# Decay, rate and gate products and head sums of an RWKV-7 block: full-precision products exchanged for products of split parts

## The chip, the cores and the metric

The program runs on one core of a Trainium2 chip. The metric is the time of one execution on the device, in microseconds. The engines are TensorE (PE, with its weight loads listed apart as PEld), VectorE (DVE), ScalarE (ACT), GpSimd (POOL) and SyncE (SP), which issues most transfers. Each engine takes its instructions strictly in the order in which they stand in its queue.

## The reference

Two transformer blocks on 256 tokens of width 2048, in float32: the first with RWKV-7 time mixing, a causal multi-scale pooling path, a feed-forward part and a gated side input, the second with gated linear attention, sparse attention and a feed-forward part. The change touches only these lines of the first block:

```python
w = -jax.nn.softplus(-(w0 + jnp.tanh(zw) @ w_up)) - 0.5      # decay, rank 64
decay = jnp.exp(-jnp.exp(w))
a = jax.nn.sigmoid(a0 + za @ a_up)                           # rate, rank 64
g = jax.nn.sigmoid(zg) @ g_up                                # gate, rank 160
...
y = wkv7_scan(r_h, hs(decay), k_h, v_h, -kk, kk * a_h)       # state 64x64 a head, 16 heads
...
y = y + jnp.sum(r_h * k_h * r_k, axis=-1, keepdims=True) * v_h
return y.reshape(B, T, RWKV_WIDTH) * g, v_first
```

## The kernel before

**Main products in split parts.** Every large weight is read in pieces of 128x1024 f32 ("halves" here: eight 128x128 blocks). `stream` (L236 to L246) takes such a piece from one of five `raw` slots (tile r), into which SyncE loads it, casts it on ACT to the reduced type fp32r (L241, tile h, one of three `hi` slots) and subtracts on DVE what was lost (L245, tile l, one of three `lo` slots; in the time-mix stage every eighth subtraction goes to POOL). Activations are split likewise (xh, xl). `gemm_a` (L251 to L267) then makes three products for each block, at L263, L264 and L265: h with xh, h with xl, l with xh. A half is thus 24 products of 128x128 weights with 256 columns. A slot comes free when its last reader is done, and slots are given out in a fixed order that the scheduler sets when the program is built; so is the order of every engine's queue.

**The time-mix stage** (`block1_mix`) first makes the three tiles of low-rank activations (`rwkv_lora`: wa of 64 decay rows over 64 rate rows, and sg of 128 and 32 gate rows), then walks over eight tiles of 128 channels (two heads each). For a tile, `rwkv_front` makes the r, k and v products (six halves) and the head norm, multiplies the small decay and rate weights (`lora`, 64 rows each) with wa in full f32 at L361 by the helper `mm`, and sums r*k over each head by a product of the constant `same` with rkk, also f32. For every pair of tiles, `rwkv_inverse` makes 31 dependent pairs of DVE steps (L524 a product xt, L526 an addition to X) between transfers through device memory, and ends with a transpose (L539) and some small products; `rwkv_chain` walks over four chunks (small products at L361, L582 and L585, copies on ACT, the update of S on DVE at L588). `rwkv_post` normalises Y, multiplies the small gate weights (`lorag`, 128 rows and 32 rows) with sg in f32 into a bank of `acc` that stays reserved for it, and writes the split result. The order of these pieces is written in `block1_mix`: the inverse and chain of one pair stand beside the main products of the next tiles, and the last pair beside the pooling path (`pool_path`, L640 to L651), which has eight tiles of main products of its own.

**Small weights.** Before, `lora` and `lorag` have buffers of their own, two each, filled by transfers that ACT issues (L402 and L599).

Of the kernel before, what the change touches and what calls it, by code (L numbers as in the profile page):

```python
# [10 lines left out]
F32 = mybir.dt.float32  # L11
F32R = mybir.dt.float32r
# [8 lines left out]
T = 256  # L21
# [81 lines left out]
def arrays_of(inputs):  # L103
    f = np.float32
    g = {k: np.asarray(v) for k, v in inputs.items()}
# [13 lines left out]
    lora = np.zeros((8, 128, 384), f)  # L119
    lora[:, :64, :128] = g["w_up"][0].reshape(64, 8, 128).transpose(1, 0, 2)  # L120
    lora[:, 64:, :128] = g["a_up"][0].reshape(64, 8, 128).transpose(1, 0, 2)
    lora[:, :, 128:256] = g["g_up"][0][:128].reshape(128, 8, 128).transpose(1, 0, 2)
    lora[:, :32, 256:384] = g["g_up"][0][128:].reshape(32, 8, 128).transpose(1, 0, 2)
# [46 lines left out]
class Kern:  # L170
# [51 lines left out]
    def head_rsqrt_rows(self, psum, pool, r):  # L222
        nc = self.nc
        x = pool.tile([128, 2, 2, 64], F32, name="hx", tag="hx")
# [153 lines left out]
    def rwkv_lora(self, act):  # L378
# [4 lines left out]
        wa = self.shifted(L, first[0], self.p("mu_wa"), "wa", bufs=1)  # L383
        nc.scalar.activation(wa[:64], wa[:64], AF.Tanh)
        sg = []
        for q in range(2):
            z = self.shifted(L, first[1 + q], self.p("mu_g", q), f"g{q}", bufs=1)
            nc.scalar.activation(z, z, AF.Tanh, scale=0.5)
            nc.vector.tensor_scalar(z, z, 0.5, 0.5, ALU.mult, ALU.add)
            sg.append(z)  # L390
        self.wa, self.sg = wa, sg
# [6 lines left out]
    def rwkv_front(self, j, act):  # L398
        nc, w = self.nc, self.I["w_in"]
        F, S = self.fp, self.store  # L400
        lora = F.tile([128, 128], F32, name="lora", tag="lora", bufs=2)
        nc.scalar.dma_start(lora, self.I["lora"][j, :, :128])  # L402
# [58 lines left out]
        inv = self.head_rsqrt_rows(self.fr, F, hr)  # L461
# [18 lines left out]
        self.mm(ps[:, :T], self.c("same"), rkk)  # L480
# [111 lines left out]
    def rwkv_post(self, tiles, mix, bank=None):  # L592
# [4 lines left out]
        for i, d in enumerate(tiles):  # L597
            lora = C.tile([128, 256], F32, name="lorag", tag="lorag", bufs=2)
            nc.scalar.dma_start(lora, self.I["lora"][d["j"], :, 128:])  # L599
            loras.append(lora)  # L600
            Y8 = d["Y"][64:].rearrange("p c h i -> p (c h) i")
            sq = C.tile([128, 8, 64], F32, name="psq", tag="psq")
# [5 lines left out]
        for i, d in enumerate(tiles):  # L608
            j, Y, lora = d["j"], d["Y"], loras[i]
# [8 lines left out]
            y = C.tile([128, T], F32, name="y", tag="y")  # L618
# [829 lines left out]
```

## Time and profile before

| | us |
|---|---|
| median of 3 runs | 2444.03 |
| lowest and highest of them | 2443.96 and 2447.99 |
| the profiled execution, its own time | 2445.46 |
| the profiled execution, span of the trace | 2443.7 |

The span runs from the first to the last instruction that the trace holds, and the execution's own time has 1.8 us around it. In the trace a busy time is the sum of the instructions of an engine, overlaps counted once; a row of a group gives how many there were, their sum and the mean of one, and then how long the engine was idle ahead of them and what ended that. PE's products are pipelined, so the length of one in the trace (0.28 us for 128x256) is longer than the distance from one start to the next, and it is the distance that counts. A product in full f32 has two records (x2), one in the split type has one.

### The profile page before, as it was taken

Reading aid. Unit: us, or ns where it says so; the run is one execution under the profiler, and the core shown is the slowest. Engines: PE = TensorE matmul, PEld = TensorE weight load, DVE = VectorE, ACT = ScalarE, POOL = GpSimd, SP = SyncE. Lnnn points to the kernel's source line nnn. Section 1 sums busy time; section 2 is a strip of 40 time slices with the busy share of each in tenths; the row PEclk is TensorE's granted clock in tenths of the full one; section 3 lists DMA queues with packets and bytes.
Section 4 is the critical chain, followed back from the end, with each engine's and each line's share of the span. In section 5 each row is a group of like instructions: output and inputs, shape, how many; then the busy total and the mean of one; then the engine's idle time right before and its main releaser. Section 6 shows DMA issues by size and latency. Waiting matters only on the chain.

```text
span 2443.7 us, 33752 instructions
## 1 busy us (share of the span) xinstructions
PE 2419.5 (99%) x12882; PEld 2045.0 (84%) x12882; DVE 1515.5 (62%) x2313; ACT 1160.4 (47%) x1654; POOL 200.0 (8%) x323
## 2 busy tenths in 40 slices
PE   9999999999999999999999999999999999999999
PEld 8988878888888888888888798888888888888887
DVE  7788866555555555556676577865555455555555
ACT  5554445444444444444565466545443434444443
POOL 1543320000000000000000044200000000000000
PEclk9999999999999999999999999999999999999999
DMA  6443336555555555556556543255555555555554
GB/s 231 159 134 113 107 103 239 185 185 190 189 190 190 189 189 190 190 188 237 183 185 237 193 149 121 94 192 185 187 189 197 183 196 189 190 190 189 190 191 162
DMA packets 135378, 439.14 MB, mean 180 GB/s; under 512 B 26784, under 2 KB 29216, under 8 KB 134064
## 3 DMA queue, kind: packets, MB, share of 16 engines
q1 hardware_dynamic: 130032, 423.58, 51.8%
q10 hardware_dynamic: 5184, 13.41, 1.4%
q8 instruction: 101, 1.65, 0.3%
q14 instruction: 61, 0.50, 0.1%
HBM read 429.59 MB, written 7.34 MB: 179 GB/s over the span
## 4 chain that ended last, share of the span: by engine, by line
PE 95%; DVE 3%; ACT 1%; issue 1%; DMA 0%; POOL 0%; SPq 0%; ACTq 0%; DVEq 0%
PE acc L741 24%; PE acc L740 24%; PE acc L742 24%; PE acc L263 4%; PE acc L264 4%; PE acc L265 4%; PE ch L361 3%; PE fr L361 2%; PE fr L879 1%; DVE l L245 1%; PE fr L782 1%; PE acc L361 1%; PE ch L582 0%; PE ch L585 0%; DVE xt L524 0%
## 5 line engine op out<-in xcount | busy, mean ns | idle before, releaser
L245 DVE TENSOR_TENSOR l<-r,h 128x1024 fp32r<-128x1024 f32 x774 | 951.6, 1230 | 772.1 <-ACT h L241 768.7
L241 ACT CAST h<-r 128x1024 fp32r<-128x1024 f32 x780 | 820.1, 1052 | 977.6 <-PE acc L742 813.9
L741 PE MATMUL acc<-l,qh 128*128 128x512 f32 x1472 | 579.4, 394 | 0.0
L742 PE MATMUL acc<-h,ql 128*128 128x512 f32 x1472 | 574.7, 390 | 0.0
L740 PE MATMUL acc<-h,qh 128*128 128x512 f32 x1472 | 521.6, 392 | 0.0
L741 PE MATMUL acc<-l,xh 128*128 128x512 f32 x1120 | 438.9, 392 | 0.0
L742 PE MATMUL acc<-h,xl 128*128 128x512 f32 x1120 | 436.7, 390 | 0.0
L740 PE MATMUL acc<-h,xh 128*128 128x512 f32 x1120 | 396.3, 391 | 0.0
L742 PEld LDWEIGHTS acc<-h,ql 128*128 128x128 f32 x1472 | 277.2, 188 | 56.3
L741 PEld LDWEIGHTS acc<-l,qh 128*128 128x128 f32 x1472 | 277.0, 188 | 56.3
L740 PEld LDWEIGHTS acc<-h,qh 128*128 128x128 f32 x1472 | 275.3, 188 | 57.2 <-issue 0.2
L741 PEld LDWEIGHTS acc<-l,xh 128*128 128x128 f32 x1120 | 210.4, 188 | 43.6
L742 PEld LDWEIGHTS acc<-h,xl 128*128 128x128 f32 x1120 | 210.5, 188 | 42.7
L740 PEld LDWEIGHTS acc<-h,xh 128*128 128x128 f32 x1120 | 209.7, 188 | 42.9
L265 PE MATMUL acc<-xh,l 128*128 128x256 f32 x512 | 149.2, 291 | 0.8 <-DVE l L245 0.6
L264 PE MATMUL acc<-xl,h 128*128 128x256 f32 x512 | 149.2, 291 | 0.0
L263 PE MATMUL acc<-xh,h 128*128 128x256 f32 x512 | 148.4, 290 | 0.0
L265 PE MATMUL acc<-qh,l 128*128 128x256 f32 x416 | 120.9, 291 | 0.2 <-DVE l L245 0.2
L263 PE MATMUL acc<-qh,h 128*128 128x256 f32 x416 | 121.2, 291 | 0.0
L264 PE MATMUL acc<-ql,h 128*128 128x256 f32 x416 | 120.7, 290 | 0.0
L265 PEld LDWEIGHTS acc<-xh,l 128*128 128x128 f32 x512 | 98.5, 192 | 3.5 <-DVE l L245 1.2
L263 PEld LDWEIGHTS acc<-xh,h 128*128 128x128 f32 x512 | 98.5, 192 | 2.9 <-issue 1.7
(424 smaller groups left out, 2256.8 us busy)
## 6 DMA issues: line engine op xcount, KB each, us to landing
r<-w_ffn_up SPq DMA_DIRECT2D x128, 512.0 KB, 3.2
r<-w_ffn_down SPq DMA_DIRECT2D x128, 512.0 KB, 3.2
r<-w_gate SPq DMA_DIRECT2D x88, 512.0 KB, 3.3
r<-w_up SPq DMA_DIRECT2D x88, 512.0 KB, 3.2
r<-w_down SPq DMA_DIRECT2D x88, 512.0 KB, 3.2
r<-w_in SPq DMA_DIRECT2D x70, 512.0 KB, 3.3
r<-w_out SPq DMA_DIRECT2D x64, 512.0 KB, 3.3
r<-w_in_2a SPq DMA_DIRECT2D x58, 512.0 KB, 3.3
```

Source lines behind the costliest of these rows:

```text
L241: nc.scalar.copy(h, r)
L245: eng.tensor_sub(l, r, h.bitcast(F32))
L263: nc.tensor.matmul(o, wh, xh, start=k == 0, stop=False)
L264: nc.tensor.matmul(o, wh, xl, start=False, stop=False)
L265: nc.tensor.matmul(o, wl, xh, start=False, stop=k == n - 1)
L361: self.nc.tensor.matmul(out, lhsT, rhs, start=start, stop=stop)
L740: nc.tensor.matmul(ps[t], ah, wh, start=first and k == 0, stop=False)
L741: nc.tensor.matmul(ps[t], ah, wl, start=False, stop=False)
L742: nc.tensor.matmul(ps[t], al, wh, start=False, stop=last and k == nk - 1)
L782: nc.tensor.transpose(ps[:, o:o + 128], self.x[:, t, kk * 128:kk * 128 + 128], self.c("ident"))
L879: nc.tensor.transpose(ps[:, o:o + 128], cols[t][:, (k + a) * 128:(k + a) * 128 + 128], self.c("ident"))
```

## The change

It does four things, all in the time-mix stage.

1. The decay and rate products become split products that use all 128 contraction rows. In device memory each small weight stands twice, one copy under the other. In `rwkv_lora`, wa is split once into hi and lo, for both placements; the one with its halves swapped is made by two transfers between partitions (tile tw). A product then has [w hi; w lo] as weights and first the hi, then the lo part as activation.
2. The gate products: for the 128 rows three split products as in a main product, for the 32 rows one product, with hi, lo and hi of the weights on three groups of 32 rows against hi, hi and lo of the activation.
3. The head sums: rkk is split (ACT and DVE), and `same` (as fp32r) multiplied with both parts.
4. Buffers: `lora` and `lorag` have none of their own any more. Their weights are loaded by ACT into a `raw` slot (now L424 and L629), cast by ACT into an `hi` slot (L459 and L641), and the lo part is subtracted by DVE into the same slot (L463, L642, L643). The split wa, sg and `same` take the room of what was freed, and several scratch tiles share places (wa with r, sg with k and v, hx with sq, y with psq). The transposes of Y are tied behind the gate products by `after`.

In the changed kernel the lines of the code behind an edit have other numbers: the main cast is L243, the main subtraction L247, and the main products are L265 to L267.

```diff
-    lora = np.zeros((8, 128, 384), f)
...
+    lora = np.zeros((8, 128, 512), f)
+    for q in range(2):
+        lora[:, q * 64:q * 64 + 64, :128] = g["w_up"][0].reshape(64, 8, 128).transpose(1, 0, 2)
+        lora[:, q * 64:q * 64 + 64, 128:256] = g["a_up"][0].reshape(64, 8, 128).transpose(1, 0, 2)
+    lora[:, :, 256:384] = g["g_up"][0][:128].reshape(128, 8, 128).transpose(1, 0, 2)
+    for q in range(3):
+        lora[:, q * 32:q * 32 + 32, 384:512] = g["g_up"][0][128:].reshape(32, 8, 128).transpose(1, 0, 2)
...
@@ rwkv_lora
-        wa = self.shifted(L, first[0], self.p("mu_wa"), "wa", bufs=1)
+        F = self.fp
+        wa = self.shifted(F, first[0], self.p("mu_wa"), "r", bufs=1)
         nc.scalar.activation(wa[:64], wa[:64], AF.Tanh)
+        turned = F.tile([128, T], F32, name="tw", tag="sq")
+        for q in range(2):
+            nc.scalar.dma_start(turned[64 * q:64 * q + 64], wa[64 * (1 - q):64 * (2 - q)])
+        self.wa = []
+        for q in range(2):
+            x = L.tile([128, 2, T], F32R, name="wa", tag=f"wa{q}")
+            for e in range(2):
+                rows = slice(64 * e, 64 * e + 64)
+                self.split(x[rows, 0], x[rows, 1], (wa if e == q else turned)[rows])
+            self.wa.append(x)
...
-        self.wa, self.sg = wa, sg
+        h0, l0, self.sg1 = (L.tile([128, T], F32R, name="sg", tag=t) for t in ("sg0h", "sg0l", "sg1"))
+        self.split(h0, l0, sg[0])
+        self.sg0 = h0, l0
+        g1, z = self.sg1, sg[1]
+        for q in (1, 2):
+            nc.scalar.dma_start(z[32 * q:32 * q + 32], z[:32])
+        nc.scalar.copy(g1, z)
+        nc.vector.tensor_sub(g1[64:96], z[64:96], g1[64:96].bitcast(F32))
+        self.same = L.tile([128, 128], F32R, name="same", tag="same")
+        nc.scalar.copy(self.same, self.c("same"))
...
@@ rwkv_front
-        lora = F.tile([128, 128], F32, name="lora", tag="lora", bufs=2)
-        nc.scalar.dma_start(lora, self.I["lora"][j, :, :128])
+        lraw = self.raw.tile([128, 1024], F32, name="r", tag="r")[:, :256]
+        nc.scalar.dma_start(lraw, self.I["lora"][j, :, :256])
...
+        lora = self.hi.tile([128, 1024], F32R, name="h", tag="h")[:, :256]
+        nc.scalar.copy(lora, lraw)
         for q, bias in ((0, self.h_w0), (1, self.h_a0)):
             ps = self.fr.tile([128, 512], F32, name="fr", tag="fr")
-            self.mm(ps[:, :T], lora[q * 64:(q + 1) * 64, :128], self.wa[q * 64:(q + 1) * 64])
+            w, low = lora[:, q * 128:q * 128 + 128], slice(64 * (1 - q), 64 * (2 - q))
+            nc.vector.tensor_sub(w[low], lraw[low, q * 128:q * 128 + 128], w[low].bitcast(F32))
+            self.mm(ps[:, :T], w, self.wa[q][:, 0], True, False)
+            self.mm(ps[:, :T], w, self.wa[q][:, 1], False, True)
...
-        self.mm(ps[:, :T], self.c("same"), rkk)
+        rh, rl = (F.tile([128, T], F32R, name="rkk" + t, tag=t) for t in ("sq", "e_end"))
+        self.split(rh, rl, rkk)
+        self.mm(ps[:, :T], self.same, rh, True, False)
+        self.mm(ps[:, :T], self.same, rl, False, True)
...
@@ rwkv_post
-            lora = C.tile([128, 256], F32, name="lorag", tag="lorag", bufs=2)
-            nc.scalar.dma_start(lora, self.I["lora"][d["j"], :, 128:])
-            loras.append(lora)
+            lraw = self.raw.tile([128, 1024], F32, name="r", tag="r")[:, :256]
+            nc.scalar.dma_start(lraw, self.I["lora"][d["j"], :, 256:])
+            loras.append(lraw)
...
+            lora = self.hi.tile([128, 1024], F32R, name="h", tag="h")
+            nc.scalar.copy(lora[:, :256], lraw)
+            nc.vector.tensor_sub(lora[:, 256:384], lraw[:, :128], lora[:, :128].bitcast(F32))
+            nc.vector.tensor_sub(lora[32:64, 128:256], lraw[32:64, 128:], lora[32:64, 128:256].bitcast(F32))
...
-            self.mm(ps[:, T:], lora[:, :128], self.sg[0], True, False)
-            self.mm(ps[:, T:], lora[:, 128:], self.sg[1], False, True)
+            self.mm(ps[:, T:], lora[:, :128], self.sg0[0], True, False)
+            self.mm(ps[:, T:], lora[:, :128], self.sg0[1], False, False)
+            self.mm(ps[:, T:], lora[:, 256:384], self.sg0[0], False, False)
+            last = nc.tensor.matmul(ps[:, T:], lora[:, 128:256], self.sg1, start=False, stop=True)
             for c in range(4):
-                nc.tensor.transpose(ps[:, c * 64:c * 64 + 64], Y[64:, c].rearrange("p h i -> p (h i)"),
-                                    self.c("ident")[64:, 64:])
+                m = nc.tensor.transpose(ps[:, c * 64:c * 64 + 64], Y[64:, c].rearrange("p h i -> p (h i)"),
+                                        self.c("ident")[64:, 64:])
+                self.after(m, last)
```

How the change moves the instructions is seen in the queues, as the built programs have them. **The first place** is ACT's queue near the end of the walk over the tiles, where the squares of Y are made. Before, it reads (L241 is the main cast, L495 and L499 belong to the front, L577, L580 and L590 to the chain, L603 is the square):

```order
L241 CAST h<-r 128x1024
L495 COPY BKt<-fr 128x512
L499 COPY UV<-fr 64x512
L590 COPY Y<-ch 64x128
L580 COPY ql<-ch 64x128
L603 ACTIVATE psq<-Y 64x512
L241 CAST h<-r 128x1024
L590 COPY Y<-ch 64x128
L603 ACTIVATE psq<-Y 64x512
```

With the change it reads (L243 is the main cast, L629 the load of a gate weight into a raw slot, L577 and L583 belong to the inverse, L607 to the chain):

```order
L243 CAST h<-r 128x1024
L629 DMA r<-lora 128x256
L529 COPY UV<-fr 64x512
L251 CAST rkksq<-rkk 128x256
L629 DMA r<-lora 128x256
L577 COPY E<-ch 32x256
L243 CAST h<-r 128x1024
L583 COPY G<-ch 32x8x32
L577 COPY E<-ch 32x256
L629 DMA r<-lora 128x256
L243 CAST h<-r 128x1024
L607 COPY rhs<-ch 64x128
```

The last row but one is the last main cast for some time: the next one stands 72 rows further on. The casts of the gate weights into hi slots (L641) stand at 8 places in the queue, six of them between these two main casts.

**The second place** is DVE's queue at the same part of the program. Before, a main subtraction (L245) stands among and right behind the inverse steps of this pair (L524, L526), with the pooling path's products (L640, L648) already under way:

```order
L526 TENSOR_TENSOR X<-X,xt 128x8x2
L524 TENSOR_TENSOR xt<-X,N 128x8
L526 TENSOR_TENSOR X<-X,xt 128x8
L640 TENSOR_TENSOR u<-acc,rb 128x256
L245 TENSOR_TENSOR l<-r,h 128x1024
L519 COPY X<-cst 128x256
L648 SCALAR_TENSOR_TENSOR pd<-us,u 128x256
L640 TENSOR_TENSOR u<-acc,rb 128x256
L539 STREAM_TRANSPOSE x_3486<-ql 32x256
L604 TENSOR_REDUCE pss<-psq 64x8
```

With the change a main subtraction (now L247) stands early in the inverse steps of one pair (L554, L556):

```order
L354 TENSOR_TENSOR z<-acc,rb 128x256 x2
L556 TENSOR_TENSOR X<-X,xt 128x28
L247 TENSOR_TENSOR l<-r,h 128x1024
L554 TENSOR_TENSOR xt<-X,N 128x54
L359 SCALAR_TENSOR_TENSOR z<-d,cols,z 128x256
L556 TENSOR_TENSOR X<-X,xt 128x2x27
L658 TENSOR_TENSOR y<-y,acc 128x256
```

and the next one stands 157 rows further on in the listing (164 instructions, since a row can hold two), among the inverse steps of the next pair and the updates of S (L618):

```order
L554 TENSOR_TENSOR xt<-X,N 128x76
L556 TENSOR_TENSOR X<-X,xt 128x4x19
L554 TENSOR_TENSOR xt<-X,N 128x72
L556 TENSOR_TENSOR X<-X,xt 128x4x18
L618 SCALAR_TENSOR_TENSOR S<-S,pc,ch 64x64 x2
L247 TENSOR_TENSOR l<-r,h 128x1024
L554 TENSOR_TENSOR xt<-X,N 128x68
L618 SCALAR_TENSOR_TENSOR S<-S,pc,ch 64x64 x2
L247 TENSOR_TENSOR l<-r,h 128x1024
L556 TENSOR_TENSOR X<-X,xt 128x4x17
```

Between these two places DVE's queue holds inverse steps, gate and chain work and no main subtraction.

**The third place** is PE's queue. Before, the products of chain, front and main stream (L263 to L265) stand mixed (lines with z,lora are the decay and rate products):

```order
L264 MATMUL acc<-xl,h 128x256
L265 MATMUL acc<-xh,l 128x256
L361 MATMUL ch<-S,AR 128x128
L361 MATMUL ch<-UV,G 64x64 x2
L263 MATMUL acc<-xh,h 128x256
L264 MATMUL acc<-xl,h 128x256
L265 MATMUL acc<-xh,l 128x256
L361 MATMUL fr<-cst,sq 128x2 x2
L361 MATMUL fr<-z,lora 128x256
L263 MATMUL acc<-xh,h 128x256
L264 MATMUL acc<-xl,h 128x256
L265 MATMUL acc<-xh,l 128x256
```

With the change the main products (L265 to L267) end at one place, 1296 of 128x256 after the program's start,

```order
L267 MATMUL acc<-xh,l 128x256
L265 MATMUL acc<-xh,h 128x256
L266 MATMUL acc<-xl,h 128x256
L267 MATMUL acc<-xh,l 128x256
L363 MATMUL fr<-cst,sq 128x2 x2
L363 MATMUL ch<-S,AR 128x128
L363 MATMUL ch<-UV,G 64x64 x2
L363 MATMUL fr<-wa,h 128x256 x2
L612 MATMUL ch<-ql 64x64 x2
L615 MATMUL ch<-ql,qh 128x128
L363 MATMUL acc<-sg,h 128x256 x3
```

and come back here, 162 products later (L363 and L650 with sg are gate products, those with wa decay and rate, L612 and L615 the chain):

```order
L612 MATMUL ch<-UV,ql 64x64 x2
L615 MATMUL ch<-UV,qh 128x128
L363 MATMUL fr<-sg,h 128x256
L363 MATMUL ch<-rhs,G 64x64 x2
L650 MATMUL fr<-sg,h 128x256
L265 MATMUL acc<-xh,h 128x256
L266 MATMUL acc<-xl,h 128x256
L612 MATMUL ch<-UV,G 64x64 x2
```

What stood before in short runs between main products stands here in one piece.

## Rows read from the trace of the kernel before

**Rows 1.** The page's head: span, and busy time of each engine (share) xinstructions.

```profile
span 2443.7 us, 33752 instructions
...
PE 2419.5 (99%) x12882; PEld 2045.0 (84%) x12882; DVE 1515.5 (62%) x2313; ACT 1160.4 (47%) x1654; POOL 200.0 (8%) x323
```

**Rows 2.** Stretches: PE, PEld, DVE, ACT, POOL busy us (xinstructions); granted clock, DMA share, GB/s.

```profile
140.00:180.00 40.00, 37.31 (x314) 33.42 (x313) 33.54 (x97) 17.90 (x33) 17.07 (x25) 0.96 0.49 149
...
220.00:260.00 40.00, 40.00 (x356) 34.92 (x355) 34.48 (x104) 20.76 (x47) 13.81 (x23) 1.00 0.36 114
```

**Rows 3.** Timeline of PE from 88.5 us: start us, us, instruction xcount.

```profile
88.33 0.28 PE L263 MATMUL acc<-xh,h 128*128 128x256 f32 x1
88.45 0.28 PE L264 MATMUL acc<-xl,h 128*128 128x256 f32 x1
...
88.69 0.28 PE L263 MATMUL acc<-xh,h 128*128 128x256 f32 x1
88.81 0.59 PE L361 MATMUL fr<-rkk,cst 128*128 128x256 f32 x2
...
89.36 0.28 PE L265 MATMUL acc<-xh,l 128*128 128x256 f32 x1
```

**Rows 4.** PE groups, 0 to 900 us: tiles xcount | busy us, mean ns | idle before.

```profile
L361 PE MATMUL fr<-z,lora 64*128 64x256 f32 x32 | 11.1, 428 | 1.9 <-DVE hm L434 1.9
L361 PE MATMUL acc<-z,lorag 128*128 128x256 f32 x24 | 6.4, 387 | 0.0
L361 PE MATMUL fr<-rkk,cst 128*128 128x256 f32 x16 | 4.9, 385 | 0.0
L361 PE MATMUL fr<-z,lorag 128*128 128x256 f32 x8 | 2.4, 405 | 0.0
```

**Rows 5.** Timeline of PE from 246.2 us.

```profile
247.55 0.70 PE L361 MATMUL fr<-z,lora 64*128 64x256 f32 x2
248.17 1.13 PE L361 MATMUL acc<-z,lorag 128*128 128x256 f32 x4
```

**Rows 6.** Groups of ACT and DVE by line, 235 to 300 us; columns as rows 4.

```profile
L241 ACT CAST h<-r 128x1024 fp32r<-128x1024 f32 x11 | 11.5, 1048 | 8.1 <-PE acc L264 8.1
L245 DVE TENSOR_TENSOR l<-r,h 128x1024 fp32r<-128x1024 f32 x10 | 12.3, 1231 | 1.0 <-ACT h L241 0.8
L524 DVE TENSOR_TENSOR xt<-X,N 128x60 f32<-128x60 f32 (+24 forms) x42 | 11.0, 262 | 0.9
L526 DVE TENSOR_TENSOR X<-X,xt 128x60 f32<-128x60 f32 (+24 forms) x41 | 10.0, 244 | 0.9
L588 DVE SCALAR_TENSOR_TENSOR S<-S,pc,ch 64x64 f32<-64x64 f32 x14 | 3.9, 279 | 3.2 <-PE ch L585 3.1
L648 DVE SCALAR_TENSOR_TENSOR pd<-us,u 128x256 f32<-128x256 f32 x4 | 2.1, 524 | 0.0
L640 DVE TENSOR_TENSOR u<-acc,rb 128x256 f32<-128x256 f32 x4 | 1.6, 419 | 2.5 <-PE acc L265 2.5
```

**Rows 7.** The same stretch as a whole.

```profile
235.00:300.00 65.00, 65.00 (x548) 56.75 (x546) 54.18 (x167) 31.32 (x67) 21.92 (x48) 1.00 0.35 109
```

**Rows 8.** Timeline from 271 us, SPq the DMA issues of SyncE.

```profile
271.10 0.17 DVE L526 TENSOR_TENSOR X<-X,xt 128x8 f32<-128x8 f32 x1
...
278.17 0.43 DVE L539 STREAM_TRANSPOSE x<-ql 32x256 f32<-32x256 f32 x1 [0.55 <-DMA ql<-xd]
```

**Rows 9.** Groups of PE, 242.4 to 295.6 us.

```profile
L264 PE MATMUL acc<-xl,h 128*128 128x256 f32 x71 | 20.7, 292 | 0.0
L263 PE MATMUL acc<-xh,h 128*128 128x256 f32 x70 | 20.7, 295 | 0.0
L265 PE MATMUL acc<-xh,l 128*128 128x256 f32 x70 | 20.3, 290 | 0.0
```

**Rows 10.** Timeline of PE from 149.5 us.

```profile
149.50 0.28 PE L265 MATMUL acc<-xh,l 128*128 128x256 f32 x1
151.69 0.70 PE L361 MATMUL fr<-z,lora 64*128 64x256 f32 x2 [1.91 <-DVE hm L434]
```

More of the change, by code (lines that the diff above doesn't have):

```diff
@@ L118, in arrays_of @@
     a["w_in"] = lay_a(np.concatenate(parts, 1), 35)
-    lora = np.zeros((8, 128, 384), f)
[L120 to L123, printed above, removed]
+    lora = np.zeros((8, 128, 512), f)
[5 more added lines that the diff above has]
+        lora[:, q * 32:q * 32 + 32, 384:512] = g["g_up"][0][128:].reshape(32, 8, 128).transpose(1, 0, 2)
     a["lora"] = lora
@@ L220, in head_rsqrt_sums, with head_rsqrt_rows @@
         return r
-    def head_rsqrt_rows(self, psum, pool, r):
+    def head_rsqrt_rows(self, psum, pool, r, place="hx"):
         nc = self.nc
-        x = pool.tile([128, 2, 2, 64], F32, name="hx", tag="hx")
+        x = pool.tile([128, 2, 2, 64], F32, name="hx", tag=place)
         nc.vector.tensor_copy(x, r.unsqueeze(3).to_broadcast([128, 2, 2, 64]))
@@ L382, in rwkv_lora @@
         self.block1_stats()
-        wa = self.shifted(L, first[0], self.p("mu_wa"), "wa", bufs=1)
+        F = self.fp
+        wa = self.shifted(F, first[0], self.p("mu_wa"), "r", bufs=1)
         nc.scalar.activation(wa[:64], wa[:64], AF.Tanh)
+        turned = F.tile([128, T], F32, name="tw", tag="sq")
[8 more added lines that the diff above has]
+            self.wa.append(x)
         sg = []
         for q in range(2):
-            z = self.shifted(L, first[1 + q], self.p("mu_g", q), f"g{q}", bufs=1)
+            z = self.shifted(F, first[1 + q], self.p("mu_g", q), "kv"[q], bufs=1)
             nc.scalar.activation(z, z, AF.Tanh, scale=0.5)
@@ L460, in rwkv_front @@
         kk = tmp("kk")
-        inv = self.head_rsqrt_rows(self.fr, F, hr)
+        inv = self.head_rsqrt_rows(self.fr, F, hr, "sq")
         nc.vector.scalar_tensor_tensor(kk, zk, self.p("k_k", j), inv, ALU.mult, ALU.mult)
@@ L597, in rwkv_post @@
         for i, d in enumerate(tiles):
-            lora = C.tile([128, 256], F32, name="lorag", tag="lorag", bufs=2)
-            nc.scalar.dma_start(lora, self.I["lora"][d["j"], :, 128:])
-            loras.append(lora)
+            lraw = self.raw.tile([128, 1024], F32, name="r", tag="r")[:, :256]
+            nc.scalar.dma_start(lraw, self.I["lora"][d["j"], :, 256:])
+            loras.append(lraw)
             Y8 = d["Y"][64:].rearrange("p c h i -> p (c h) i")
-            sq = C.tile([128, 8, 64], F32, name="psq", tag="psq")
+            sq = C.tile([128, 512], F32, name="psq", tag="psq").rearrange("p (c i) -> p c i", c=8)
             nc.scalar.activation(sq[64:], Y8, AF.Square)
@@ L612, in rwkv_post @@
             ps = bank if bank is not None else self.fr.tile([128, 512], F32, name="fr", tag="fr")
-            self.mm(ps[:, T:], lora[:, :128], self.sg[0], True, False)
-            self.mm(ps[:, T:], lora[:, 128:], self.sg[1], False, True)
+            self.mm(ps[:, T:], lora[:, :128], self.sg0[0], True, False)
+            self.mm(ps[:, T:], lora[:, :128], self.sg0[1], False, False)
+            self.mm(ps[:, T:], lora[:, 256:384], self.sg0[0], False, False)
+            last = nc.tensor.matmul(ps[:, T:], lora[:, 128:256], self.sg1, start=False, stop=True)
             for c in range(4):
-                nc.tensor.transpose(ps[:, c * 64:c * 64 + 64], Y[64:, c].rearrange("p h i -> p (h i)"),
-                                    self.c("ident")[64:, 64:])
-            y = C.tile([128, T], F32, name="y", tag="y")
+                m = nc.tensor.transpose(ps[:, c * 64:c * 64 + 64], Y[64:, c].rearrange("p h i -> p (h i)"),
+                                        self.c("ident")[64:, 64:])
+                self.after(m, last)
+            y = C.tile([128, 512], F32, name="y", tag="psq")[:, :T]
             nc.scalar.activation(y, ps[:, :T], AF.Identity, scale=self.p("gn_g", j), bias=self.p("gn_b", j))
```

2 lines of the change are left out of this document (1 added, 1 removed).

## Prediction

> **What bounds the kernel now.** I read the head of the page first: in a span of 2443.7 us the matrix engine PE is busy 99%, VectorE (DVE) 62%, ScalarE (ACT) 47% [rows 1]. So time is won by taking work from PE and lost wherever PE must wait. A busy row alone is no peak, so I then looked at the pitch of its products in the timeline: main products of 128x256 in the split type start every 0.12 us, one behind the other [rows 3]; there is no slack to win but fewer or cheaper products. Third, the sums by stretch: in the time-mix stage, where the change sits, DVE is busy 34 us of every 40 [rows 2], far more than its mean over the span. Every eight main-product weights (one "half", 24 products, 2.9 us of PE) need one cast on ACT and one subtraction on DVE, 1.23 us [rows 6]; if DVE's queue holds that subtraction back, PE stands still. That has happened once here: PE waited 1.91 us with DVE's work named as the releaser [rows 10]. So the stage has two near limits, PE and the delivery of split weights.
>
> **Part 1, the products: -7.6 us.** Removed are 16 decay/rate products, 16 gate products and 8 head sums in full f32. Each shows as two records (32, 24 + 8 and 16 in [rows 4]). The price of one is read from [rows 3]: from the start of L263 at 88.69 to the start of L265 at 89.36 lie one L263, one f32 product and one L264: 0.67 - 2 x 0.12 = 0.43 us. 40 x 0.43 = 17.2 us. Added are 32 + 32 + 16 = 80 products of the split type with 256 columns, the same form as the main products: 80 x 0.12 = 9.6 us. Saved: 7.6 us. The bound above: a 64-row product between two others of unlike shape took 248.17 - 247.55 = 0.62 us [rows 5], 0.19 more; if all 16 were such, 3.0 us more, 10.6. I take 7.6, because the order mostly sets them between main products as in [rows 3]. All of it lies on PE, the engine that sets the end.
>
> The two 64-row products of a tile take one half of the array's rows each, and each had its own 0.43 to 0.62 us [rows 3, 5]. The Trainium skill's page "TensorE: Matmul & The Clock Gate" (Why this matters for your kernels) says that products on few contraction rows run at the same time if they lie on distinct row groups; by it the 16 would have cost as much as 8, and stacking them on all rows would give up 8 x 0.43 = 3.4 us of the saving, for a sum higher by 3.4. The trace does not bear this out here: in [rows 5] the row that follows the 64-row product starts 0.62 us later, and the order sets the two of a tile far apart.
>
> **Part 2, the splitting: 0 us beside other work.** Per tile DVE gets one subtraction of 128x256 (about a quarter of the 1.23 us for 128x1024, so 0.3 to 0.4) and four of at most 128x128 (I use 0.28, the 64x64 update of [rows 6]): 1.5 us, 12 us over eight tiles; ACT gets three casts, about 1 us a tile. Both lie beside PE: DVE has 5.5 to 6.5 us free in 40 [rows 2] and a tile takes 17 to 25. If that cover were gone, up to 12 us would show; I keep that as an end. The loads of the small weights stay 16 in number; the four small copies between partitions stand at the head of the stage, where the order lets 36 more main products go ahead of the first head norm. 0 for these.
>
> **Part 3, the gap in the weight stream: +17 us.** This is the main term. The small weights no longer have buffers of their own: they are loaded into the five raw slots and cast into the three h slots of the main stream, and a gate's h slot is freed only by its gate product. The scheduler, which fills slots as they come free, lets ACT fetch six gate weights early (the ACT rows with L629) and then cast them; in its order ACT has no main cast (L243) for 71 rows, and DVE has no main subtraction (L247) between two places that are 164 instructions apart. PE has 162 small products in a row without a main one; before, the longest such run in this stage was 17. Engines take their rows in order, so PE can only wait there.
>
> How long is it? DVE: the gap holds 41 pairs of inverse steps (xt, X) and 14 updates of S. The stretch from 235 to 300 us before holds almost the same: 42, 41 and 14 [rows 6]. There DVE was busy 54.2 us [rows 7], of which 12.3 were ten main subtractions [rows 6]: 41.9. Off go pool-path steps that the gap does not hold, 2.1 + 1.6 [rows 6], on come 14 new subtractions by 0.28: about 42. Waits: the last inverse step starts at 271.10, the first transpose of its result at 278.17 [rows 8]: 6.9 us after that step's end, with about 4 us of own work in the gap to do meanwhile, so 3 us; and 3.2 us before the S updates [rows 6]. So 48 us.
>
> PE in that time: from 242.4 to 295.6 us before, the same steps of chain and inverse ran with 211 main products [rows 9]: 211 x 0.12 = 25.3 of 53.2 us, so 27.9 us for the small products, their turn-overs included. The gap has three groups of gate products more than that stretch, some 1.4 us, and no pool products; I take 28. Ahead of it lies the last half, 2.9 us. Idle: 48 - 28 - 2.9 = 17 us. Ends: below, 42 us of DVE without waits and two halves ahead, 42 - 28 - 5.8 = 8; above, no two DVE instructions overlapping (the 41 + 41 inverse steps by 0.25, 14 S by 0.28, the other 68 at 0.35 on the mean come to 49, plus 6 of waits, 55) and PE's small products at their bare pitch of some 20 us, 55 - 20 = 35. I take 17, since [rows 6, 7] are a measured stretch of nearly the same content.
>
> **Part 4, fewer slots: +4 us.** Around the gap, one h slot is held by the second gate of a pair while its bank is waited for, over some 280 main products before it and as many after: 23 halves on two slots. Cast plus subtraction plus products are 1.05 + 1.23 [rows 6] + 2.9 us against 2 x 2.9 for two slots; it fits only if neither queue is late. Below 0; above one subtraction of 1.23 a half, 28 us. Before, only the one wait of [rows 10] came from DVE in these stretches, so I take 4, two such waits.
>
> **Part 5, the clock: +2 us.** The stretch with the 1.91 us wait shows a granted clock of 0.96, its neighbours 1.00 [rows 2, 10]: 0.04 x 40 = 1.6 us. One more such stretch or two: 2, ends 0 and 5.
>
> **Sum.** The profiled run took 2445.5 us (span 2443.7 and 1.8 around it), 1.4 above the median of 2444.0. 2445.5 - 7.6 + 0 + 17 + 4 + 2 = 2460.9; I say 2461. After the gap the rest of the program (feed-forward, second block) is in the order almost unchanged, and nothing comes back there.
>
> **The rivals.** *Covered gap, faster.* The gap in the order might be short in time: DVE's inverse steps have a mean of 262 and 244 ns [rows 6] that includes some stretched by a neighbour, and without main subtractions between them they may run closer. The point from which this decides is a gap of 28 + 2.9 + 7.6 = 38.5 us on DVE; under it the saved products win. At the best it gives 2445.5 - 7.6 = 2438. Against it: 41.9 us measured for such content, before any wait. Chance 0.13. *Half covered:* a gap near 38 to 42 us, the whole within 5 us of before, about 2447; chance 0.10. *Starved slots:* part 4 at its upper end, every half on two slots late by one subtraction: 2461 - 4 + 28 = 2485. For it: DVE is already 84 to 86% busy there [rows 2], and its rows stand in a fixed order; against it: PE's small products lie between the halves and give them time. Chance 0.20. *Row groups* (the rule under part 1): 2464, chance 0.05, which lies inside the forecast's own spread. The forecast with it has 0.57.
>
> **How the numbers follow.** A change of 0.2%, 4.9 us, is about what a measurement of this kernel can tell from none. Faster by more than that needs the covered gap: 0.13. Within: the half-covered case, 0.10. Slower: the forecast and the starved slots, 0.77. The likeliest case alone spans 2449 (part 3 at 8, part 4 at 1) to 2479 (part 3 at 35); the range for 8 in 10 goes from 2444, which leaves out the covered gap, to 2486, which takes in the starved slots.
>
> **What would show it.** The changed profile should show, some 240 us into the span, a stretch of about 20 to 50 us in which PE's busy share falls and DVE's stays high, with no L247 on DVE and no L243 on ACT; its small products of 128x256 at a pitch of 0.12 us; and the clock of that stretch under 1.00. Part 3 is wrong if PE stays at 40 of 40 there. Part 1 is wrong if the new products start further apart than 0.12 us. If PE's waits are spread over the stage, on DVE l or ACT h, part 4 was too small. If the loss stands after 400 us, the whole working is wrong.

## The result, and the profile after

The changed kernel takes 2490.57 us (median of 4 runs, 2486.55 to 2491.47) against 2445.37 us of the kernel before (also 4 runs): a ratio of 1.0178, 95% interval 1.0166 to 1.0190. It is slower, as forecast, but by 45 us where 16 were forecast and 41 were the end of the range. The head of the page of its profiled run (columns as [rows 1]):

```profile
span 2489.6 us, 33877 instructions
...
PE 2437.1 (98%) x12882; PEld 2062.0 (83%) x12882; DVE 1535.5 (62%) x2359; ACT 1170.3 (47%) x1685; POOL 212.1 (9%) x323
```

PE is busy 18 us longer with cheaper products, which points to a slower PE. The sums by stretch (columns as [rows 2], to which the first two answer):

```profile
140.00:180.00 40.00, 35.79 (x304) 33.58 (x303) 35.56 (x85) 17.52 (x34) 21.66 (x29) 0.88 0.45 125
220.00:260.00 40.00, 38.21 (x329) 33.87 (x327) 35.99 (x94) 21.72 (x53) 16.61 (x23) 0.91 0.32 90
260.00:300.00 40.00, 28.48 (x188) 23.15 (x187) 27.34 (x106) 12.49 (x33) 9.23 (x17) 0.57 0.17 44
300.00:320.00 20.00, 20.00 (x130) 17.36 (x130) 13.64 (x44) 7.49 (x16) 0.00 (x0) 0.74 0.38 126
```

From 260 to 300 us PE works 28.5 of 40 us and its granted clock is 0.57, near the lower of its two levels (1.2 GHz); DVE, the expected limit, works no more than 27.3. The forecast gap is there. In PE's timeline the main products stop at 251.96 and come back at 305.26:

```profile
251.84 0.28 PE L267 MATMUL acc<-xh,l 128*128 128x256 f32 x1
251.96 0.51 PE L363 MATMUL fr<-cst,sq 128*128 128x2 f32 x4
...
304.88 0.58 PE L650 MATMUL fr<-sg,h 128*128 128x256 f32 x1
305.26 0.41 PE L265 MATMUL acc<-xh,h 128*128 128x256 f32 x1
```

The gap as a whole (sums by stretch, the same columns):

```profile
251.90:305.50 53.60, 42.06 (x284) 34.50 (x283) 39.51 (x144) 21.63 (x58) 13.20 (x22) 0.63 0.24 70
```

DVE's groups of the change from its last main subtraction (ended 243.2) to the next (304.9), which answer to [rows 6]:

```profile
L554 DVE TENSOR_TENSOR xt<-X,N 128x60 f32<-128x60 f32 (+24 forms) x41 | 10.4, 255 | 2.7 <-DMA ql<-xd 1.7
L556 DVE TENSOR_TENSOR X<-X,xt 128x60 f32<-128x60 f32 (+24 forms) x41 | 10.0, 244 | 1.0
L618 DVE SCALAR_TENSOR_TENSOR S<-S,pc,ch 64x64 f32<-64x64 f32 x14 | 3.9, 279 | 4.8 <-PE ch L615 4.7
L643 DVE TENSOR_TENSOR h<-r,h 32x128 fp32r<-32x128 f32 x6 | 3.3, 547 | 0.1
...
L634 DVE TENSOR_REDUCE pss<-psq 64x8 f32<-64x512 f32 x2 | 1.4, 683 | 3.0 <-ACT psq L633 2.9
```

The counts and durations are those of the forecast (41 pairs of steps at 255 and 244 ns); the waits are not.

**Where the 46 us lie.** I put the same place of both programs side by side, the main product of 128x512 that has 384 others ahead of it (a place in the out projection, called the mark): it comes at 453.5 us before and at 499.8 after, 46.3 us later, and at the end the two traces are 45.9 us apart. Up to the mark I added up, in stretches of 2 us, the time that PE was not busy, and the busy time times one minus the granted clock; the rest is PE's work at full clock.

| run | mark | not busy | slow clock | work | last split |
|---|---|---|---|---|---|
| before | 453.5 | 10.2 | 3.4 | 439.9 | 398.6 |
| the change | 499.8 | 37.5 | 35.9 | 426.5 | 417.9 |
| e1 | 470.1 | 19.9 | 15.0 | 435.1 | 428.9 |
| e5 | 462.6 | 14.4 | 5.0 | 443.2 | 422.8 |
| e9 | 499.0 | 34.2 | 16.9 | 447.9 | 424.3 |
| e13 | 465.4 | 21.2 | 9.3 | 434.9 | 422.6 |
| e15 | 462.0 | 22.2 | 10.0 | 429.8 | 420.6 |
| e16 | 452.3 | 12.3 | 3.4 | 436.6 | 397.4 |

"Last split" is the end of the last subtraction on DVE that writes the stage's result (in the change and e9, where the pooling path comes late, one of that path; the last of the tiles ends at 411.6 and 406.2 there). So 27 us of standing still and 32.5 us of slow clock came, and less work stands against them. That is bookkeeping: it does not say that without the slow clock 32.5 us would be saved (e9). It is also rough. The slow-clock column takes a product at half the clock to last twice as long, but the rows at the end of this document show about 1.65 times for small products, and two main products at the lower clock start 0.22 us apart (305.26 and 305.48 us) instead of 0.12; so that column is some 10 to 20% too large (an estimate from these rows), and "work" too small by as much. And "work" differs by 3 us either way among kernels that have the same products (before, e5, e16).

Not all of it lies in the gap. Of the 37.5 us that PE stands still in the change, 11.9 lie from 240 to 300 us, 9.2 from 60 to 180 (3.4 before), and 9.7 from 380 us to the mark (0.0 before), most of these in waits for a main cast (us, times, longest):

```profile
PE acc L777 <- ACT h L243: 6.3, 4, 2.1
```

### The profile page after: what moved, and what is told of

Read it like the earlier page. It is cut to its first block, busy times and chain, and to the rows that moved or that the text cites. A ratio compares the mean times of both kernels' runs of the same rounds, so it can differ in the third digit from the quotient of the medians.

```text
span 2489.6 us, 33877 instructions
## 1 busy us (share of the span) xinstructions
PE 2437.1 (98%) x12882; PEld 2062.0 (83%) x12882; DVE 1535.5 (62%) x2359; ACT 1170.3 (47%) x1685; POOL 212.1 (9%) x323
## 3 DMA queue, kind: packets, MB, share of 16 engines
q8 instruction: 101, 1.65, 0.3%
## 4 chain that ended last, share of the span: by engine, by line
PE 91%; DVE 6%; ACT 1%; DMA 1%; issue 1%; SPq 0%; POOL 0%; ACTq 0%; DVEq 0%
PE acc L778 24%; PE acc L777 24%; PE acc L779 24%; PE acc L267 3%; PE acc L266 3%; PE acc L265 3%; PE ch L363 3%; DVE l L247 1%; PE fr L363 1%; PE fr L916 1%; PE fr L819 1%; DVE X L556 0%; PE acc L363 0%; PE ch L612 0%; DVE xt L554 0%
## 5 line engine op out<-in xcount | busy, mean ns | idle before, releaser
L247 DVE TENSOR_TENSOR l<-r,h 128x1024 fp32r<-128x1024 f32 x774 | 951.0, 1229 | 786.0 <-ACT h L243 779.1
L243 ACT CAST h<-r 128x1024 fp32r<-128x1024 f32 x780 | 819.8, 1052 | 964.1 <-PE acc L779 823.6
L777 PEld LDWEIGHTS acc<-h,xh 128*128 128x128 f32 x1120 | 209.7, 188 | 42.9
L267 PE MATMUL acc<-xh,l 128*128 128x256 f32 x512 | 152.9, 299 | 7.5 <-DVE l L247 7.4
L265 PE MATMUL acc<-xh,h 128*128 128x256 f32 x512 | 150.2, 293 | 0.0
L266 PE MATMUL acc<-xl,h 128*128 128x256 f32 x512 | 149.5, 292 | 0.0
L267 PE MATMUL acc<-qh,l 128*128 128x256 f32 x416 | 120.5, 290 | 0.2 <-DVE l L247 0.2
L265 PE MATMUL acc<-qh,h 128*128 128x256 f32 x416 | 120.5, 290 | 0.0
L267 PEld LDWEIGHTS acc<-xh,l 128*128 128x128 f32 x512 | 100.8, 197 | 10.7 <-DVE l L247 9.2
L265 PEld LDWEIGHTS acc<-xh,h 128*128 128x128 f32 x512 | 101.0, 197 | 1.3
```

Of the source, the lines that this page charges most:

```text
L243: nc.scalar.copy(h, r)
L247: eng.tensor_sub(l, r, h.bitcast(F32))
L265: nc.tensor.matmul(o, wh, xh, start=k == 0, stop=False)
L266: nc.tensor.matmul(o, wh, xl, start=False, stop=False)
L267: nc.tensor.matmul(o, wl, xh, start=False, stop=k == n - 1)
L777: nc.tensor.matmul(ps[t], ah, wh, start=first and k == 0, stop=False)
```

## The experiments

**Which part makes the gap.** e1 gives the gate weights buffers of their own. For room, x11 and E are merged into one tile and rkk laid on zd.

```diff
-lraw = self.raw.tile([128, 1024], F32, name="r", tag="r")[:, :256]
+lraw = C.tile([128, 256], F32, name="lorag", tag="lorag", bufs=1)
-lora = self.hi.tile([128, 1024], F32R, name="h", tag="h")
+lora = C.tile([128, 384], F32R, name="lh", tag="lh", bufs=1)
-x11 = R.tile([32, 2, 4, 32], F32, name="x11", tag="x11")
+E = R.tile([64, 2, 4, 32], F32, name="E", tag="E")
+x11 = E[0:32]
```

> The changed kernel with all its split products, but the gate weights in buffers of their own (one of 1 KB for the load, one of 1.5 KB for hi and lo parts); the room comes from laying x11 and E into one tile and rkk and zd into one place. Theory A (the gate weights in the main stream's raw and hi slots make the gap, and the gap makes idle time and a low clock): the gap of 162 products is gone from the order, PE has no stretch with a clock under 0.9 after 200 us, and the time is 2436 to 2450 us. Theory B (the added splitting on DVE and ACT is what PE waits for): all of that work is still there, so 2475 us or more.

2464.25 us, ratio 1.0067 (1.0052 to 1.0083). The slow stretch went (clock 1.00 from 180 to 300 us; what is left of it, about 0.75, lies at 340 to 380), but the time stayed between the two theories, and a clock under 0.9 after 200 us is a miss for theory A too. e2 is its control, the merged places alone.

> Control for e1: the changed kernel with only the scratch tiles merged (x11 with E, rkk with zd), the gate weights still in the shared slots. Both theories: about as slow as the changed kernel, 2480 to 2510 us, with the gap and the slow stretch at 250 to 310 us still there (the order has 207 small products in a row here).

2493.32 us, 1.0185 (1.0168 to 1.0202). e3 has no split product of the change at all:

```diff
-lora = C.tile([128, 256], F32, name="lorag", tag="lorag", bufs=2)
+lora = self.raw.tile([128, 1024], F32, name="r", tag="r")[:, :256]
...
+lora = self.hi.tile([128, 1024], F32, name="h", tag="h")[:, :256]
+nc.scalar.copy(lora, lraw)
```

> The kernel before with full-precision products throughout; only the gate weights are loaded into a raw slot and copied by ACT into an hi slot, as the change does it. Theory A: the gap appears without any split product, 2470 to 2505 us, the clock at half in part of 250 to 310 us. Theory B: nothing of the splitting is there, so 2440 to 2450 us.

2483.12 us, 1.0145 (1.0130 to 1.0160), with the low clock in the same place (sums by stretch of e3):

```profile
240.00:260.00 20.00, 19.55 (x94) 15.07 (x93) 14.93 (x52) 9.85 (x27) 7.80 (x10) 0.61 0.17 54
260.00:300.00 40.00, 34.98 (x252) 27.71 (x250) 27.32 (x98) 15.23 (x42) 6.78 (x15) 0.68 0.23 63
```

So the buffers alone, with products untouched, cost 35 us: shown. e4 undoes the gate part (products as in the kernel before, two buffers `lorag`) and keeps the rest; x11 and E are merged in it as in e1.

> The changed kernel with its gate part undone (full-precision gate products, two buffers of their own), decay, rate and head sums still in split products and their small weights still in shared slots. Theory A: no gap, 24 of 40 products exchanged, so 2445 - 24 x 0.43 + 48 x 0.12 = 2440 us, 2437 to 2450 with some waits left. Theory B: only the gate's DVE work (16 subtractions of 0.28 us and its casts) is gone, so 2475 us or more.

2467.29 us, 1.0080 (1.0065 to 1.0095): no gap, but again some 20 us above the kernel before. Neither theory covers that.

**What the rest is.** Four steps from the kernel before, all with the merged x11 and E for room. e5 has nothing else; e6 adds the head sums in split products; e7 has instead the decay and rate products split (weights in tags e_in and cum, and scratch places shared as in the change: wa with r, hx with sq), e8 the same through raw and hi slots.

```diff
-self.mm(ps[:, :T], self.c("same"), rkk)
+self.mm(ps[:, :T], self.same, rh, True, False)
+self.mm(ps[:, :T], self.same, rl, False, True)
...
-lora = F.tile([128, 128], F32, name="lora", tag="lora", bufs=2)
+lraw = F.tile([128, T], F32, name="lora", tag="e_in")
+lora = F.tile([128, T], F32R, name="lh", tag="cum")
```

> The kernel before with x11 and E laid into one tile and nothing else: no product, cast, subtraction or load is changed, only the order of the queues moves a little. Theory A (what is left of the loss, 16 to 20 us above the kernel before in the runs without the gap, comes from added DVE work and from slots): within 5 us of before. Theory C (the queue order is set so finely here that any small change moves the tail of the time-mix stage by 10 us or more): off by more than 5 us, either way.

2454.62 us, 1.0036 (1.0020 to 1.0051).

> The kernel before (with x11 and E in one tile for room) and only the head sums in split products: 8 x (0.43 - 2 x 0.12) = 1.5 us less on PE, 8 subtractions of 0.42 us more on DVE, no slot of the stream taken. Theory A: at most 3.4 us of DVE more, so 2441 to 2450 us. Theory C: as far off as e5 is, the sign open. The small gain itself can't be told from no change.

2459.89 us, 1.0055 (1.0040 to 1.0070).

> The kernel before and only the decay and rate products in split parts, their small weights in scratch places of the front (e_in and cum), so that no slot of the stream is taken. PE: 16 x (0.43 - 2 x 0.12) = 3.0 us less; DVE: 16 subtractions of 0.29 us more, 4.6 us. Theory A with the loss in the slots: 2438 to 2448 us. Theory A with the loss in the DVE work: 2448 to 2460. Theory C: anything from 2440 to 2470, with no relation to e8.

2465.78 us, 1.0079 (1.0062 to 1.0096).

> As e7, but the small weights go through a raw slot and an hi slot of the main stream, as in the change. Theory A with the loss in the slots: 8 us or more above e7, with waits of PE for l (L245) or of ACT for a slot spread over the stage. Theory A with the loss in the DVE work: within 4 us of e7. Theory C: differs from e7 by more than 5 us, either way.

2459.25 us, 1.0054 (1.0039 to 1.0069). The shared slots of decay and rate cost nothing here, rather less than the scratch places of e7. e5 to e7 lie above theory A's ranges, and e8 is neither 8 us above e7 nor within 4 of it. e6 and e8 stand some 5 us above e5, not clear of it, and e7 11 us, clear of it. e5 looked like theory C, but its trace names a cause. DVE's timeline of the kernel before has these transposes at the end of the second inverse:

```profile
209.97 0.43 DVE L539 STREAM_TRANSPOSE x<-G 32x256 f32<-32x256 f32 x1 [0.95 <-DMA G<-xd]
222.76 0.43 DVE L539 STREAM_TRANSPOSE x<-ql 32x256 f32<-32x256 f32 x1 [2.02 <-PE ch L545]
```

The same view of e5:

```profile
213.62 0.42 DVE L540 STREAM_TRANSPOSE E<-G 32x256 f32<-32x256 f32 x1
231.31 0.43 DVE L540 STREAM_TRANSPOSE E<-ql 32x256 f32<-32x256 f32 x1 [0.49 <-PE ch L551]
```

In one tile the second x11 must wait until the first E is used up: 17.7 us apart instead of 12.8 here, and 8.8, 16.5 and 12.0 instead of 3.4, 3.2 and 9.2 at the other pairs; the last split comes at 422.8 instead of 398.6, and the mark 9.1 us later (DVE's timelines of the kernel before and of e5):

```profile
398.20 0.43 DVE L250 TENSOR_TENSOR ql<-y,qh 128x256 fp32r<-128x256 f32 x1 [0.89 <-ACT qh L249]
422.38 0.43 DVE L250 TENSOR_TENSOR ql<-y,qh 128x256 fp32r<-128x256 f32 x1 [0.88 <-ACT qh L249]
```

Is the chain of the four pairs of tiles (inverse, chain, gate, one behind the other) then a second end beside PE's products? In the eleven runs without the gap whose last split ends from 420.6 to 440.0 us, the mark comes 39.3 to 42.9 us behind it; in the kernel before and in e12 and e16, whose last split ends by 400.3, it comes 54.9 us behind. It looks as if the chain had had 14 us to spare before. But PE has a nearly fixed number of products of 128x512 between the two, 154 to 170 in the eleven traces and 230 in the three, and from 380 us to the mark it never stands still in e1, e8, e10, e14 and e15 (1.0 us in e13, 3.1 to 3.7 in e4 to e7 and e11). So a late chain holds PE up there in some of the runs at most, and by no more than that; that it sets the end is not shown, and neither are the 14 us. PE around the last split of e1, at 428.9 us (sums by stretch):

```profile
400.00:420.00 20.00, 20.00 (x93) 15.74 (x92) 12.53 (x22) 8.43 (x11) 0.00 (x0) 1.00 0.54 183
420.00:440.00 20.00, 20.00 (x93) 16.22 (x94) 11.43 (x15) 11.58 (x19) 2.50 (x2) 1.00 0.77 268
```

**Clock and DVE.** e9 keeps PE at work in the gap by products that nothing reads; e10 moves the subtractions that the change adds to POOL, on e1; e11 is e10 with `share = 6`, e12 the kernel before with `share = 6`.

```diff
+if d["j"] in (2, 3):
+    for _ in range(10):
+        nc.tensor.matmul(ps[:, 256:512], self.same, self.sg1, start=True, stop=True)
...
-nc.vector.tensor_sub(lora[:, 256:384], lraw[:, :128], lora[:, :128].bitcast(F32))
+nc.gpsimd.tensor_sub(lora[:, 256:384], lraw[:, :128], lora[:, :128].bitcast(F32))
```

> The changed kernel with products added whose result nothing reads: ten of 128x256 in split type at each step of the chain of tiles 2 and 3, and twenty before each gate of tiles 2 to 5; 147 of them stand in the gap (309 small products in a row instead of 162), 17.6 us at 0.12 us each. Theory D (the low clock lengthens the gap, since in it the chain's small products and the work that waits for them run at half speed): the fillers keep PE at work, the clock in 250 to 310 us is above 0.9 for the most part, and in spite of the added products the kernel is not slower than the change, 2476 to 2490 us. Theory E (DVE alone sets the length of the gap, the clock is only a companion): the clock may rise but the time doesn't fall, 2490 to 2505 us.

2494.82 us, 1.0199 (1.0176 to 1.0222). The clock rose (sums by stretch of e9):

```profile
240.00:260.00 20.00, 20.00 (x166) 17.77 (x164) 19.03 (x78) 9.97 (x28) 6.23 (x9) 1.00 0.22 73
260.00:300.00 40.00, 35.61 (x298) 30.55 (x296) 26.37 (x96) 14.13 (x41) 8.65 (x17) 0.79 0.15 38
```

The slow clock fell from 35.9 to 16.9 us in the table, the work rose by 21.4, and the gap closed no earlier (main products come back at 308.3 us, 305.3 in the change). The time lies in theory E's range. Since the added products also stood in front of the chain's, it is not shown that the clock cost nothing; it is shown that giving half of it back this way wins nothing.

> As e1 (all split products, gate weights in their own buffers) and all the subtractions that the change adds go to POOL instead of DVE: per tile one of 128x256 and four smaller ones, some 2 us of DVE a tile by the rows of e1, 15 us in all. Theory F (what is left of the loss in e1, 16.6 us, is DVE: at its limit around 120 to 260 us it delays the last pair of tiles, whose chain then runs with little main work beside it): the last split of the stage ends before 415 us (429 in e1, 398.6 before), and the time is 2440 to 2455 us. Theory C (the order alone, which any small change shuffles): no relation to DVE's load, anything from 2445 to 2475 us.

2455.59 us, 1.0036 (1.0021 to 1.0051), some 8 us under e1 by the ratios, and clear of it; last split 422.5, later than the 415 that theory F wanted. The time is just above its range.

> As e10, and every sixth main subtraction of the stage instead of every eighth goes to POOL, some three more by 1.23 us off DVE, by 2.4 us onto POOL. Theory F: at or below e10, 2436 to 2455 us, the last split not later than in e10. Theory C: off from e10 by more than 5 us either way.

2469.48 us, 1.0093 (1.0078 to 1.0108). A miss for F: two more main subtractions on POOL (8 in the trace instead of 6), and the order that the scheduler makes of it, are all that differs from e10, and why they cost 14 us was not followed up.

> The kernel before with every sixth instead of every eighth main subtraction of the stage on POOL, nothing else. Theory F says that DVE's load matters here too: 2440 to 2447 us. Theory C: as the run with the merged scratch tiles, which changed nothing either and came out 8 us above, 2449 to 2462 us.

2448.41 us, 1.0006 (0.9997 to 1.0015). Between the ranges of F (to 2447) and C (from 2449), and no change that can be told from none: a reshuffled order alone did not cost 4 us here. It may have cost 14 in e11.

**Without my own merged tile.** e13 is e1 with x11 and E apart (room from k2 laid on z_v); e14 has them in one tile with two buffers, e15 also the subtractions on POOL; e16 is the kernel before with the double tile.

```diff
-k2 = tmp("k2")
+k2 = F.tile([128, T + 1], F32, name="k2", tag="z_v")[:, 1:]
...
+E = R.tile([64, 2, 4, 32], F32, name="E", tag="E", bufs=2)
```

> As e1 (all split products, gate weights in their own buffers), but x11 and E are two tiles again as in the change; the room comes from laying rkk on zd and k2 on z_v. Theory G (the merged tile of x11 and E, which all runs from e1 to e11 that made room carry, makes the two tiles of a pair finish their inverse one after the other: in e5 that alone moved the last split of the stage from 398.6 to 422.8 us and the time by 8): the last split is at 400 to 416 us, and the time 2445 to 2456 us. Theory C (the order alone): as e1, 2460 us or more, or unrelated.

2458.89 us, 1.0056 (1.0040 to 1.0073): 32 us under the change, with the clock back (sums by stretch of e13),

```profile
240.00:260.00 20.00, 19.89 (x184) 17.76 (x179) 16.78 (x47) 9.36 (x21) 6.25 (x8) 1.00 0.35 109
260.00:300.00 40.00, 39.50 (x319) 34.89 (x318) 36.23 (x102) 20.66 (x48) 16.77 (x38) 1.00 0.35 100
```

but the last split at 422.6, later than the 400 to 416 expected, and the time above theory G's range. Against e1 the gain is 3 us by the ratios and not clear of noise: the 8 us that the merged tile costs in the kernel before do not show here.

> As e13, with x11 and E in one tile that has two buffers, which takes no more room than two tiles: the two tiles of a pair share nothing at the end of their inverse. Theory G: the transposes (L569 in the change) of a pair come closer together than 4 to 13 us, the last split at or before that of e13, and the time 2438 to 2452 us, not above e13. Theory C: off from e13 by more than 5 us either way.

2459.03 us, 1.0055 (1.0039 to 1.0071). The transposes stood 0.7 to 2.2 us apart, and nothing came of it: last split 428.3, later than in e13, and a time above theory G's range.

> As e14, with the added subtractions on POOL as in e10. Theory G with DVE as the second limit: another 3 to 9 us less, 2434 to 2448 us, at or below the kernel before. Theory C: unrelated to e14.

2454.97 us, 1.0037 (1.0022 to 1.0053), not clear of e14 and above the range of theory G, which thus missed in all three.

> The kernel before with x11 and E in one tile with two buffers, nothing else. The chain of pairs gets shorter, but the kernel before has some 15 us between the end of that chain and the point where it would set the end (in the slower runs the 384th product of 512 columns comes about 40.5 us after the last split, in the kernel before 55). Theory G: the last split earlier than 398 us, and 2440 to 2447 us, no change. Theory C: 2449 us or more.

2446.44 us, 1.0007 (0.9997 to 1.0016): as theory G had it (last split 397.4), and with e5 the proof that one buffer for that tile was the cost in the kernel before.

**Which pool.** e17 is e13 with the loads in raw slots again, e18 with hi and lo parts in hi slots again.

> As e13, but only the hi and lo parts of the gate weights have a buffer of their own; they are still loaded into the raw slots of the main stream. If it is the hi slots that make the gap: as e13, 2452 to 2464 us. If the raw slots alone are enough (a gate weight sits in one from its early load until its cast): a gap of some 200 small products and 2480 to 2505 us. The order, which has 205 small products in a row here, speaks for the second.

2490.35 us, 1.0182 (1.0167 to 1.0197).

> As e13, but only the loads of the gate weights have buffers of their own (two); their hi and lo parts are still in the hi slots of the main stream. If it is the raw slots that make the gap: as e13, 2452 to 2464 us. If the hi slots alone are enough: 185 small products in a row, as the order has it, and 2480 to 2505 us. Both runs slow would mean that each of the two shared pools makes the gap by itself.

2497.01 us, 1.0210 (1.0193 to 1.0227). Each of the two pools makes the gap by itself (sums by stretch, first e17, then e18):

```profile
260.00:300.00 40.00, 36.52 (x229) 30.58 (x228) 27.58 (x104) 14.63 (x40) 10.05 (x18) 0.54 0.16 37
260.00:300.00 40.00, 35.92 (x252) 29.54 (x252) 31.05 (x115) 17.11 (x49) 10.81 (x19) 0.63 0.15 34
```

The main products stay away from 240.7 to 306.0 us in e17 and from 257.9 to 313.6 in e18. No version beat the kernel before.

## Why the prediction was wrong in size

**Part 1 held in its price.** The new products follow the main ones at 0.12 us, in PE's timeline two of them in 0.25:

```profile
60.73 0.28 PE L267 MATMUL acc<-xh,l 128*128 128x256 f32 x1
60.84 0.40 PE L363 MATMUL fr<-wa,h 128*128 128x256 f32 x2
61.09 0.28 PE L265 MATMUL acc<-xh,h 128*128 128x256 f32 x1
```

PE's work up to the mark is 5.0 us less in e13, against the 7.6 reckoned; with the 3 us by which that column differs between equal products, it neither bears out the 7.6 nor speaks against it.

**Part 3, +17 us: right in kind, too small.** The place, the 41 pairs of steps and PE's small work were right (42.06 us busy at a clock of 0.63 are 26.5 at full clock, or up to 29 if the lower clock costs what the rows at the end of this document show; I had 28). The wrong number is DVE's hole, 48 us reckoned and 61.7 measured: I took its waits from a stretch where PE ran at full clock beside main products [rows 7, 8], 6 us, and they were 16 (60.8 less 44.6 busy in the sums below, of DVE's hole in the change). In the gap the engines wait for each other in a ring, DVE for PE (L618), for ACT (L634), PE for DVE. Put into the forecast's own sum, the measured hole gives 61.7 - 28 - 2.9 = 31 us, and undoing the gap is worth 2490.57 - 2458.89 = 32 us. That the upper end of 35 took this in is luck: it was reckoned from a hole of 55 us and 20 us of PE's work, and both are off (its 49 us of DVE work, added up again, are 48).

```profile
243.20:304.00 60.80, 49.26 (x328) 41.09 (x327) 44.60 (x162) 24.13 (x65) 15.18 (x25) 0.64 0.22 63
```

With 32 in place of 17 the forecast's sum would be 2476, still inside its range; the rest up to 2490.57 is the other parts.

**Part 5, the clock, +2 us: wrong as a term.** The table has 32.5 us more of slow clock (too large by a tenth to a fifth, as said); the price of one short wait [rows 2, 10] says nothing of a gap in which PE has only small products. What it costs on its own stays open (e9); part of it stands in the 32 us. Without the gap, in e13, the column still grows by 5.9 us, most of it from 340 to 360 us, where the clock is 0.74 and PE works 18.01 of 20 us.

**Part 2, the splitting at 0 us, wrong, and part 4, +4 us, right in kind.** They and part 1 make -3.6, and e13, which has all of this and no gap, is 13.5 us above the kernel before. I had named DVE as the cover and kept 12 us for its failing as an end, but judged it by free time in 40 us. From 60 to 240 us DVE is busy 9 to 12 us longer and PE 6 to 7 us less (sums by stretch; before, the change, e13):

```profile
60.00:240.00 180.00, 176.58 (x1470) 163.36 (x1470) 151.27 (x384) 90.80 (x167) 78.89 (x117) 0.99 0.43 134
60.00:240.00 180.00, 169.15 (x1409) 158.54 (x1407) 162.89 (x400) 92.63 (x179) 84.42 (x119) 0.96 0.41 127
60.00:240.00 180.00, 170.20 (x1417) 159.89 (x1416) 160.34 (x385) 93.24 (x175) 82.94 (x115) 0.98 0.44 139
```

PE waits for l in that stretch (us, times, longest; before, then the change):

```profile
PE acc L265 <- DVE l L245: 0.6, 1, 0.6
PE acc L267 <- DVE l L247: 7.4, 8, 2.3
```

In e13 these waits are 5.6 us, which is about what part 4 had, and another 2.4 us are one wait for the lo part of rkk, which part 2 had at nothing. By the table e13's mark comes 11.9 us later than before: 11.0 of standing still and 5.9 of slow clock more, 5.0 of work less. Of the standing still, 6.4 come from 60 to 180 us and 2.7 from 300 to 380 us.

What I also missed is the chain of the pairs. The first inverse step of the four pairs begins 8.9, 16.1, 15.4 and 20.7 us later in e13 than before (at 124.8 us instead of 115.9 in the first), and the last split 24 us. How much of e13's loss comes from the late chain and how much from the waits before it, no run separates. The subtractions are part of it: with them on POOL e10 is clear of e1, though e15 is not clear of e14, and PE's waits for l did not shrink (8.3 us in e10, 6.1 in e1). What else delays the last split by 22 us in e15 is not settled; the scratch places that the change lets share and its added casts on ACT stand in every one of these runs and were not tested alone.

**The rivals.** The covered gap fell. Row groups: no run bears on it, and the 0.62 us [rows 5] do not either, since the two 64-row products of a tile are never neighbours. Starved slots, 2485, came nearest in time, but the main loss is one gap and not waits spread over the stage, though 7.4 us of those are there, more than part 4 had, as its sign of being wrong said.

## What to carry to other kernels

Weights that are read late and rarely did badly in the slots of a stream here: they are fetched early, hold a slot until their turn, and the stream stands; either of two shared pools was enough, and the harm can be read in the order of the queues. Before pricing work as hidden by a mean of free time, look for the places where the busy engine already waits for the engine that is to hide it: one wait of 0.6 us for l became eight. Follow the slowest dependent chain too; a scratch tile with one buffer too few moved its end by 24 us and cost 8. And two instants that keep their distance from run to run need not be cause and effect: count first what the order puts between them. An experiment that needs room needs a control with that room alone.

## What was not expected of the hardware

PE's granted clock stayed at 0.50 in stretches in which PE counted as busy throughout: from 270 to 278 us of the change it was busy 8.0 of 8 us. PE's timeline of the change has the same chain products twice, at a clock of 1.00 and of 0.50:

```profile
252.72 0.44 PE L363 MATMUL ch<-UV,G 64*64 64x64 f32 x4
253.09 0.51 PE L363 MATMUL fr<-wa,h 128*128 128x256 f32 x2
...
271.29 0.69 PE L363 MATMUL ch<-UV,G 64*64 64x64 f32 x4
271.90 0.69 PE L612 MATMUL ch<-ql 128*64 128x64 f32 x4
```

The four records of ch<-UV,G take 0.37 us to the next row in the first place and 0.61 in the second, 1.65 times as long at half the clock. A busy share of 100% did not go with a high clock; with filler products among them it was 1.00 from 250 to 280 us (e9).
